# The second group of each ConvFFN: its up projection as seven block products instead of two direct tiles

## The chip, the cores and the metric

The kernel runs on one core of one Trainium2 chip. The metric is the device time of one execution in microseconds; the runs of a kernel are told by their median.

## What is computed

A two-layer decoder trunk on 512 tokens of width 1024, in float32. Each layer adds a mixer and then a gated ConvFFN to the residual stream. The ConvFFN is what the change touches:

```python
def gated_conv_ffn(x, w_gate, w_up, conv_w, conv_b, w_down):
    g = jnp.einsum('bsd,df->bsf', x, w_gate)          # 1024 -> 2816
    g = causal_dwconv3(g, conv_w) + conv_b            # width 3, along the tokens
    up = jnp.einsum('bsd,df->bsf', x, w_up)           # 1024 -> 2816
    return jnp.einsum('bsf,fd->bsd', jax.nn.silu(g) * up, w_down)

for layer in range(2):
    h = h + mixer(rms_norm(h, norm_mix[layer]))
    hn = rms_norm(h, norm_ffn[layer])
    h = h + gated_conv_ffn(hn, w_ffn_gate[layer], w_ffn_up[layer], ...)
return rms_norm(h, final_norm)
```

## The kernel before

**Precision.** Every float32 operand of a matmul is held as a high and a low part, and each product is three matmuls: high by high, high by low, low by high (`mm3`, lines 139 to 141; line 631 for block products). The high part is a rounding copy on ScalarE. The low part is source minus high: a subtraction on VectorE (`parts`, lines 134 and 135; `halves`, lines 640 and 641), or ScalarE writes the negated high part and a DMA from POOL's queue adds the source to it (`summed`, lines 126 to 128; lines 602 to 604 in `normalize`).

**Groups and parts.** The hidden width 2816 is 22 tiles of 128 columns. A group `f` is two neighbouring tiles of the gate and of the up projection. Groups 0 and 2 are followed by the down projection of tiles 0 and 1 (called `d` in layer 0, `dn` in layer 1); groups 4, 6, 8 and so on follow, with a down projection of four tiles behind every one or two groups, as `PARTS` says. The activations of group 2 are thus used one part later.

**Group 0** (`hidden(0)`) starts before the norm's root is known: it multiplies by the input scaled with the gain alone, tile by tile over the 8 blocks of 128 input channels in the order `PAIRS` (0, 4, 1, 5, 2, 6, 3, 7), and its results are multiplied by the root when they leave PSUM. In the middle of it TensorE sums the squares (`rstd_tokens`) and spreads the root over the partitions by four transposes (`rstd_spread`, line 211; ScalarE's copy is line 214). Then `normalize(kp)`, for the four pairs of input blocks (kp, kp + 4), writes the normalized input over `hg` and makes four combinations `t` of its quarters (lines 579 to 604). Their high and low parts are `t23` and `t41`. `rest()` then evacuates group 0: root, convolution (one scaled copy on ScalarE, line 512, two steps on VectorE, line 514), silu (line 520), multiplication with up (line 569), split into `a_hi` and `a_lo` (lines 253 and 255).

**Group 2** is direct too, on the normalized input: the gate's two tiles first, then the two up tiles, 48 matmuls of 512 columns each. Its weights come through `pair_weights`.

**Groups from 4 on** (`both`) use Strassen's scheme in its seven-product form. The matrix of 1024 input channels by two tiles is cut in halves both ways, and so is the input (channel half by token half). Seven block products, each 4 x 3 matmuls of 256 columns (`multiply`), replace eight. Each needs a stationary block of the weights or a combination of them (`a11` for product 1, `s12` for 5 and 6, `s34` for 7 and 3, the lower half of the weights for 2 and 4) and a moving block of the input or of its combinations: products 6 and 7 read `t23`, 4 and 5 read `t41`. The products are added partly in PSUM and partly in `kept` or in padded rows.

**What sets the order.** A framework takes the program's order as priority and orders every engine's instructions itself when the kernel is built. Buffers turn round in pools: four for raw weights (`raw`), six each for high and low parts (`whi`, `wlo`), three for sums (`sum`), seven PSUM banks for matmuls (`mm`) and one beside (`aux`). A tile waits for a buffer until all readers of an earlier one are done. Loads of weights go through SP's queue.

Of the kernel before, what the change touches and what calls it, by code (L numbers as in the profile page):

```python
# [8 lines left out]
F32 = mybir.dt.float32  # L9
# [3 lines left out]
ALU = mybir.AluOpType  # L13
PSUM = bass.MemoryType.PSUM

P = 128
D = 1024
S = 512
NK = D // P
# [11 lines left out]
def tile_trunk(ctx: ExitStack, tc: tile.TileContext, x, norm_mix, norm_ffn, final_norm,  # L31
# [3 lines left out]
    nc = tc.nc  # L35
    x = x[0]
# [8 lines left out]
    def mm_bank(name):  # L45
        return ps_mm.tile([P, 512], F32, tag="mm", name=name)
# [91 lines left out]
    def mm3(ps, lhs, rhs, start, stop):  # L138
        nc.tensor.matmul(ps, lhs[0], rhs[0], start=start, stop=False)  # L139
        nc.tensor.matmul(ps, lhs[0], rhs[1], start=False, stop=False)  # L140
        nc.tensor.matmul(ps, lhs[1], rhs[0], start=False, stop=stop)  # L141
# [27 lines left out]
    def hg_k(k):  # L169
        return hg[k][0], hg[k][1]  # L170

    class Norm:
# [6 lines left out]
        def add(self, k):  # L179
            g = self.gain(k)  # L180
            nc.scalar.activation(hg[k][0], h[k], AF.Copy, scale=g)
            nc.vector.scalar_tensor_tensor(hg[k][1], h[k], g, hg[k][0].bitcast(F32),
                                           op0=ALU.mult, op1=ALU.subtract)
            self.square(k)
# [90 lines left out]
    def padded_tile():  # L275
        turn[0] += 1
        return padded[turn[0] % NPADDED]
# [205 lines left out]
    HALF = S // 2  # L483
    NP = NK // 2
    PAIRS = [k for i in range(NP) for k in (i, i + NP)]

    def ffn_weights(layer, f, order):
        cs = slice(f * P, (f + 2) * P)
        return {(key, half): fetch(
            (w_ffn_gate if key == "g" else w_ffn_up)[layer][half * 512 : (half + 1) * 512, cs]  # L490
            .rearrange("(k p) c -> p k c", p=P), 4, 256, f"{key}{layer}_{f}_{half}")
            for key, half in order}

    class Ffn:
# [42 lines left out]
                ch[key, half] = (summed if key in by_dma else parts)(raw, 4, 2 * P, name)  # L537
            return ch

        def direct(self, f, normed, sets, ch, before=lambda i, j: None):  # L540

            layer = self.layer
            banks = {}
            for js in sets:
                for i, k in enumerate(PAIRS):
                    for j in js:
                        before(i, j)
                        hi, lo = ch["gu"[j // 2], i // 4]
                        c = slice((j % 2) * P, (j % 2 + 1) * P)
                        if j not in banks:  # L550
                            banks[j] = mm_bank(f"gu{layer}_{f}_{j}")
                        mm3(banks[j], (hi[:, i % 4, c], lo[:, i % 4, c]), hg_k(k),
                            i == 0, i == NK - 1)

            def evacuate():
                r = self.r
                gates = []
                for j in range(2):
                    t = padded_tile()
                    if normed:  # L560
                        nc.scalar.copy(t[:, 2:], banks[j])
                    else:
                        nc.vector.tensor_tensor(t[:, 2:], banks[j], r, ALU.mult)
                    s = self.silu(self.conv(t, f + j), f + j)
                    if not normed:
                        nc.gpsimd.tensor_tensor(s, s, r, ALU.mult)
                    gates.append(s)
                for j, s in enumerate(gates):
                    nc.vector.tensor_tensor(s, banks[2 + j], s, ALU.mult)
                    self.act(f + j, s)  # L570

            return evacuate

        def normalize(self, kp):

            n, r = f"{self.layer}_{kp}", self.r
            x = self.ap.tile([P, 2, S], F32, tag="sum", bufs=3, name=f"x{n}")
            for i, k in enumerate((kp, kp + NP)):
                nc.vector.scalar_tensor_tensor(x[:, i, :], h[k], self.prm("ffn", k), r,
                                               op0=ALU.mult, op1=ALU.mult)  # L580

            def halves(dst, src):
                nc.scalar.activation(dst[0], src, AF.Copy)
                nc.vector.tensor_tensor(dst[1], src, dst[0].bitcast(F32), ALU.subtract)

            halves(hg[kp], x[:, 0, :])
            halves(hg[kp + NP], x[:, 1, :])
            b11, b12 = x[:, 0, :HALF], x[:, 0, HALF:]
            b21, b22 = x[:, 1, :HALF], x[:, 1, HALF:]
            t = self.ap.tile([P, 4, HALF], F32, tag="sum", bufs=3, name=f"t{n}")  # L590
            nc.vector.tensor_tensor(t[:, 1, :], b22, b12, ALU.subtract)
            nc.vector.tensor_tensor(t[:, 0, :], t[:, 1, :], b11, ALU.add)
            nc.vector.tensor_tensor(t[:, 3, :], b12, b11, ALU.subtract)
            nc.vector.tensor_tensor(t[:, 2, :], b21, t[:, 0, :], ALU.subtract)
            self.t23[kp] = self.sums(kp)
            t41 = self.ap.tile([P, 2, 2, HALF], F32R, name=f"t41_{n}")
            self.t41[kp] = t41[:, 0], t41[:, 1]
            for (hi, lo), src in ((self.t23[kp], t[:, :2, :]), (self.t41[kp], t[:, 2:, :])):
                if kp < 2:
                    halves((hi, lo), src)  # L600
                    continue
                nc.scalar.activation(lo, src, AF.Copy, scale=-1.0)
                nc.gpsimd.dma_start(lo, src, accum_op=ALU.add)
                nc.scalar.activation(hi, src, AF.Copy)
# [34 lines left out]
        def halves(self, hi, lo, src):  # L639
            nc.scalar.activation(hi, src, AF.Copy)  # L640
            nc.vector.tensor_tensor(lo, src, hi.bitcast(F32), ALU.subtract)  # L641

        def both(self, f):

# [74 lines left out]
        def hidden(self, f, before=lambda i, j: None):  # L719
            if f == 0:  # L720
                def first(i, j):
                    before(i, j)
                    if (i, j) == (1, 0):
                        self.norm.rstd_tokens()
                    elif (i, j) == (2, 2):
                        self.r = self.norm.rstd_spread()

                ch = self.pair_weights(0, [("g", 0), ("u", 0), ("g", 1), ("u", 1)])
                rest = self.direct(0, False, (range(4),), ch, first)
                self.ch = self.pair_weights(2, [("g", 0), ("g", 1), ("u", 0), ("u", 1)], "g")  # L730
                for kp in range(NP):
                    self.normalize(kp)
                rest()
            elif f == 2:
                self.direct(2, True, ((0, 1), (2, 3)), self.ch)()
            else:
                self.both(f)

# [229 lines left out]
    n = mixer0()  # L968
    n = ffn0(n)
    n = mixer1(n)  # L970
# [31 lines left out]
```

## Time and profile before

| what | value |
|---|---|
| median of 3 runs | 1000.65 us (1000.1 to 1001.06) |
| the profiled execution | 1000.02 us, of it span 998.3 us |
| granted TensorE clock, mean | 0.998 |
| TensorE busy | 986.5 us (99%), 5835 matmuls |
| VectorE / ScalarE / POOL busy | 699.9 / 522.7 / 100.6 us |
| HBM read and written | 98.42 and 2.10 MB |

Times in rows are microseconds from the span's start unless marked ns. A timeline row is start, duration, engine, line, operation, output<-inputs, shape and count; in brackets stands the idle time before it and what ended it. In names the layer and buffer numbers are mostly left out: `gu` is a direct bank of groups 0 and 2, `u_4a` the bank `a` of group 4's up products, `d` and `dn` the down projections. Durations of neighbouring instructions on one engine overlap a little, so the distance between two starts is the price of one.

### The profile page before, as it was taken

Reading aid. Unit: us, or ns where it says so; the run is one execution under the profiler, and the core shown is the slowest. Engines: PE = TensorE matmul, PEld = TensorE weight load, DVE = VectorE, ACT = ScalarE, POOL = GpSimd, SP = SyncE. Lnnn points to the kernel's source line nnn. Section 1 sums busy time; section 2 is a strip of 40 time slices with the busy share of each in tenths; the row PEclk is TensorE's granted clock in tenths of the full one; section 3 lists DMA queues with packets and bytes.
Section 4 is the critical chain, followed back from the end, with each engine's and each line's share of the span. In section 5 each row is a group of like instructions: output and inputs, shape, how many; then the busy total and the mean of one; then the engine's idle time right before and its main releaser. Section 6 shows DMA issues by size and latency. Waiting matters only on the chain.

```text
span 998.3 us, 14727 instructions
## 1 busy us (share of the span) xinstructions
PE 986.5 (99%) x5835; PEld 874.5 (88%) x5835; DVE 699.9 (70%) x1057; ACT 522.7 (52%) x775; POOL 100.6 (10%) x117
## 2 busy tenths in 40 slices
PE   8999999999999999999999999999999999999997
PEld 6888888898999989999888888888989899898995
DVE  5977457967785877858943645389668868688677
ACT  6522345744653746537655444675536366363663
POOL 3032030300000000000300001202000010000100
PEclk9999999999999999999999999999999999999999
DMA  7532225454554645546433223434535446354442
GB/s 233 184 105 85 85 85 127 107 150 124 130 145 106 175 121 132 144 106 184 132 127 106 63 86 104 100 91 118 158 95 145 141 112 184 94 141 146 119 115 84
DMA packets 81904, 124.53 MB, mean 125 GB/s; under 512 B 4292, under 2 KB 53676, under 8 KB 81836
## 3 DMA queue, kind: packets, MB, share of 16 engines
q1 hardware_dynamic: 73580, 98.96, 31.6%
q0 software_dynamic: 6912, 23.07, 12.9%
q10 hardware_dynamic: 1344, 1.58, 0.5%
q8 instruction: 45, 0.74, 0.3%
q14 instruction: 23, 0.19, 0.1%
HBM read 98.42 MB, written 2.10 MB: 101 GB/s over the span
## 4 chain that ended last, share of the span: by engine, by line
PE 92%; DVE 4%; DMA 2%; ACT 1%; issue 0%; SPq 0%; POOL 0%; DVEq 0%; ACTq 0%; POOLq 0%
PE d L139 4%; PE d L140 4%; PE d L141 4%; PE dn L139 4%; PE dn L140 3%; PE dn L141 3%; PE gu L139 3%; PE gu L141 3%; PE gu L140 3%; PE u L141 1%; PE oo L141 1%; PE oo L139 1%; PE u L140 1%; PE u L139 1%; PE oe L140 1%; PE oe L139 1%
## 5 line engine op out<-in xcount | busy, mean ns | idle before, releaser
L139 PE MATMUL dn<-whi_dn,a_hi 128*128 128x512 f32 x176 | 68.7, 390 | 0.0
L140 PE MATMUL d<-a_lo,whi_d 128*128 128x512 f32 x176 | 68.6, 390 | 0.0
L140 PE MATMUL dn<-wlo_dn,a_hi 128*128 128x512 f32 x176 | 68.6, 390 | 0.0
L141 PE MATMUL d<-a_hi,wlo_d 128*128 128x512 f32 x176 | 68.5, 389 | 0.0
L514 DVE SCALAR_TENSOR_TENSOR c<-rows,prm,c 128x512 f32<-128x512 f32 x88 | 67.5, 791 | 0.0
L141 PE MATMUL dn<-whi_dn,a_lo 128*128 128x512 f32 x176 | 67.3, 390 | 0.0
L139 PE MATMUL d<-a_hi,whi_d 128*128 128x512 f32 x176 | 66.9, 390 | 0.0
L127 POOL DMA_DIRECT2D wlo_g<-raw_g x22 | 19.1, 868 | 382.3 <-ACT wlo_g L126 350.7
L931 DVE TENSOR_TENSOR y<-dn,y 128x512 f32<-128x512 f32 x48 | 32.3, 685 | 22.8 <-PE dn L141 22.3
L126 ACT ACTIVATE wlo_g<-raw_g 128x1024 fp32r<-128x1024 f32 x22 | 23.2, 1055 | 42.4 <-PE dn L140 42.4
L135 DVE TENSOR_TENSOR wlo_u<-raw_u,whi_u 128x1024 fp32r<-128x1024 f32 x16 | 19.6, 1223 | 34.2 <-ACT whi_u L134 34.1
L520 ACT ACTIVATE s<-c,prm 128x512 f32<-128x512 f32 x44 | 30.9, 717 | 22.7 <-DVE c L514 22.6
L640 ACT ACTIVATE whi_s12u<-s12u 128x1024 fp32r<-128x1024 f32 x18 | 18.9, 1050 | 43.1 <-PE d L140 33.7
L641 DVE TENSOR_TENSOR wlo_s34u<-s34u,whi_s34u 128x1024 fp32r<-128x1024 f32 x18 | 22.1, 1226 | 26.1 <-ACT whi_s34u L640 26.1
L141 PEld LDWEIGHTS dn<-whi_dn,a_lo 128*128 128x128 f32 x176 | 33.0, 188 | 7.5 <-DVE a_lo L255 0.2
L140 PEld LDWEIGHTS d<-a_lo,whi_d 128*128 128x128 f32 x176 | 33.1, 188 | 7.2 <-DVE a_lo L255 0.2
L139 PEld LDWEIGHTS dn<-whi_dn,a_hi 128*128 128x128 f32 x176 | 33.1, 188 | 7.1 <-ACT a_hi L253 0.2
L139 PEld LDWEIGHTS d<-a_hi,whi_d 128*128 128x128 f32 x176 | 32.8, 188 | 7.0
L298 DVE TENSOR_TENSOR h<-d,h 128x512 f32<-128x512 f32 x48 | 32.5, 685 | 9.2 <-PE d L141 9.2
L141 PEld LDWEIGHTS d<-a_hi,wlo_d 128*128 128x128 f32 x176 | 33.0, 188 | 6.7
L140 PEld LDWEIGHTS dn<-wlo_dn,a_hi 128*128 128x128 f32 x176 | 33.1, 188 | 6.5
L135 DVE TENSOR_TENSOR wlo_dn<-raw_dn,whi_dn 128x1024 fp32r<-128x1024 f32 x22 | 26.8, 1221 | 12.8 <-ACT whi_dn L134 12.8
(1201 smaller groups left out, 3412.3 us busy)
## 6 DMA issues: line engine op xcount, KB each, us to landing
raw_g<-in_w_ffn_gate_dram SPq DMA_DIRECT2D x36, 512.0 KB, 4.0
raw_u<-in_w_ffn_up_dram SPq DMA_DIRECT2D x36, 512.0 KB, 4.0
wlo_g<-raw_g POOLq DMA_DIRECT2D x22, 512.0 KB, 4.8
raw_d<-in_w_ffn_down_dram SPq DMA_DIRECT2D x22, 512.0 KB, 4.4
raw_dn<-in_w_ffn_down_dram SPq DMA_DIRECT2D x22, 512.0 KB, 4.7
wlo_u<-raw_u POOLq DMA_DIRECT2D x18, 512.0 KB, 4.7
raw_oe<-in_w_out_even_dram SPq DMA_DIRECT2D x8, 512.0 KB, 3.5
raw_g<-in_w_ffn_gate_dram SPq DMA_DIRECT2D x16, 256.0 KB, 2.9
```

The source lines that it names most:

```text
L126: nc.scalar.activation(lo, raw, AF.Copy, scale=-1.0)
L127: nc.gpsimd.dma_start(lo, raw, accum_op=ALU.add)
L135: nc.vector.tensor_tensor(lo, raw, hi.bitcast(F32), ALU.subtract)
L139: nc.tensor.matmul(ps, lhs[0], rhs[0], start=start, stop=False)
L140: nc.tensor.matmul(ps, lhs[0], rhs[1], start=False, stop=False)
L141: nc.tensor.matmul(ps, lhs[1], rhs[0], start=False, stop=stop)
L298: nc.vector.tensor_tensor(h[k], ps, h[k], ALU.add)
L514: nc.vector.scalar_tensor_tensor(c, t[:, i : S + i], prm("cf", i * NF + ft), c, op0=ALU.mult, op1=ALU.add)
L520: nc.scalar.activation(s, c, AF.Silu, bias=self.prm("bf", ft))
L640: nc.scalar.activation(hi, src, AF.Copy)
L641: nc.vector.tensor_tensor(lo, src, hi.bitcast(F32), ALU.subtract)
L931: nc.vector.tensor_tensor(dst, ps, dst, ALU.add)
```

## The change

The up projection of group 2 is computed in the seven products; the gate stays direct. The new function `up_only` loads the two halves of the up weights, makes the stationary blocks (`a1` for products 1 and 2, `s12u`, `s34u`, and `a22` for 4), and then orders TensorE's work: the gate's first six input blocks, products 1 and 2, one gate block of three matmuls, products 6, 5 and 7, the gate's last nine matmuls, and products 4 and 3. The results are collected in `kept`. `direct` now serves group 0 alone. In `normalize` the low parts of `t` for pairs 2 and 3 are made on VectorE and those of pairs 0 and 1 by DMA, which is the other way round than before. The root is spread before tile (2, 0) of group 0 instead of (2, 2). `multiply`, `unit` and `moving` are the functions that the later groups use.

```diff
--- before.py
+++ after.py
@@ -537,33 +537,28 @@
                 ch[key, half] = (summed if key in by_dma else parts)(raw, 4, 2 * P, name)
             return ch
 
-        def direct(self, f, normed, sets, ch, before=lambda i, j: None):
+        def direct(self, f, ch, before):
 
             layer = self.layer
             banks = {}
-            for js in sets:
-                for i, k in enumerate(PAIRS):
-                    for j in js:
-                        before(i, j)
-                        hi, lo = ch["gu"[j // 2], i // 4]
-                        c = slice((j % 2) * P, (j % 2 + 1) * P)
-                        if j not in banks:
-                            banks[j] = mm_bank(f"gu{layer}_{f}_{j}")
-                        mm3(banks[j], (hi[:, i % 4, c], lo[:, i % 4, c]), hg_k(k),
-                            i == 0, i == NK - 1)
+            for i, k in enumerate(PAIRS):
+                for j in range(4):
+                    before(i, j)
+                    hi, lo = ch["gu"[j // 2], i // 4]
+                    c = slice((j % 2) * P, (j % 2 + 1) * P)
+                    if j not in banks:
+                        banks[j] = mm_bank(f"gu{layer}_{f}_{j}")
+                    mm3(banks[j], (hi[:, i % 4, c], lo[:, i % 4, c]), hg_k(k),
+                        i == 0, i == NK - 1)
 
             def evacuate():
                 r = self.r
                 gates = []
                 for j in range(2):
                     t = padded_tile()
-                    if normed:
-                        nc.scalar.copy(t[:, 2:], banks[j])
-                    else:
-                        nc.vector.tensor_tensor(t[:, 2:], banks[j], r, ALU.mult)
+                    nc.vector.tensor_tensor(t[:, 2:], banks[j], r, ALU.mult)
                     s = self.silu(self.conv(t, f + j), f + j)
-                    if not normed:
-                        nc.gpsimd.tensor_tensor(s, s, r, ALU.mult)
+                    nc.gpsimd.tensor_tensor(s, s, r, ALU.mult)
                     gates.append(s)
                 for j, s in enumerate(gates):
                     nc.vector.tensor_tensor(s, banks[2 + j], s, ALU.mult)
@@ -596,7 +591,7 @@
             t41 = self.ap.tile([P, 2, 2, HALF], F32R, name=f"t41_{n}")
             self.t41[kp] = t41[:, 0], t41[:, 1]
             for (hi, lo), src in ((self.t23[kp], t[:, :2, :]), (self.t41[kp], t[:, 2:, :])):
-                if kp < 2:
+                if kp >= 2:
                     halves((hi, lo), src)
                     continue
                 nc.scalar.activation(lo, src, AF.Copy, scale=-1.0)
@@ -639,6 +634,77 @@
         def halves(self, hi, lo, src):
             nc.scalar.activation(hi, src, AF.Copy)
             nc.vector.tensor_tensor(lo, src, hi.bitcast(F32), ALU.subtract)
+
+        def up_only(self, f, ch):
+
+            layer, ap, n = self.layer, self.ap, f"{self.layer}_{f}"
+            raws = ffn_weights(layer, f, [("u", 0), ("u", 1)])
+            r0, r1 = raws["u", 0][0], raws["u", 1][0]
+            stat = {}
+            w = self.unit(f"a1_{n}")
+            self.halves(w[0][:, 0], w[1][:, 0], r0[:, :, :P])
+            self.halves(w[0][:, 1], w[1][:, 1], r1[:, :, :P])
+            stat[1], stat[2] = (tuple(x[:, i] for x in w) for i in range(2))
+            s12, s34 = (ap.tile([P, 2, 4, P], F32, tag="sum", bufs=3, name=f"{x}u_{n}")
+                        for x in ("s12", "s34"))
+            nc.vector.tensor_tensor(s12[:, 0], r0[:, :, P:], r1[:, :, P:], ALU.add)
+            nc.vector.tensor_tensor(s12[:, 1], s12[:, 0], r0[:, :, :P], ALU.subtract)
+            w = self.unit(f"s12u_{n}")
+            self.halves(*w, s12)
+            stat[5], stat[6] = (tuple(x[:, i] for x in w) for i in range(2))
+            nc.vector.tensor_tensor(s34[:, 0], r0[:, :, :P], r0[:, :, P:], ALU.subtract)
+            nc.vector.tensor_tensor(s34[:, 1], r1[:, :, :P], s12[:, 1], ALU.subtract)
+            w = self.unit(f"s34u_{n}")
+            self.halves(*w, s34)
+            stat[7], stat[3] = (tuple(x[:, i] for x in w) for i in range(2))
+            w = self.unit(f"a22_{n}")
+            self.halves(w[0][:, 0], w[1][:, 0], r1[:, :, P:])
+            stat[4] = w[0][:, 0], w[1][:, 0]
+
+            banks = {}
+
+            def gate(i, js):
+                k = PAIRS[i]
+                for j in js:
+                    if j not in banks:
+                        banks[j] = mm_bank(f"g{j}{n}")
+                    hi, lo = ch["g", i // 4]
+                    c = slice(j * P, (j + 1) * P)
+                    mm3(banks[j], (hi[:, i % 4, c], lo[:, i % 4, c]), hg_k(k),
+                        i == 0, i == NK - 1)
+
+            def product(p):
+                return self.multiply(banks, f"u{n}", p, stat[p])
+
+            kept = ap.tile([P, 3, HALF], F32, tag="kept", bufs=1, name=f"kept{n}")
+
+            def add(i, ps):
+                nc.vector.tensor_tensor(kept[:, i, :], ps, kept[:, i, :], ALU.add)
+
+            for i in range(6):
+                gate(i, range(2))
+            nc.scalar.copy(kept[:, 0, :], product(1))
+            add(0, product(2))
+            gate(6, (0,))
+            nc.scalar.copy(kept[:, 1, :], product(6))
+            p5 = product(5)
+            nc.scalar.copy(kept[:, 2, :], product(7))
+            add(2, p5)
+            gate(6, (1,))
+            gate(7, range(2))
+            s = []
+            for j in range(2):
+                t = padded_tile()
+                nc.scalar.copy(t[:, 2:], banks[j])
+                s.append(self.silu(self.conv(t, f + j), f + j))
+            p4 = product(4)
+            nc.vector.tensor_tensor(s[1][:, HALF:], kept[:, 2, :], s[1][:, HALF:], ALU.mult)
+            nc.vector.tensor_tensor(s[1][:, :HALF], p4, s[1][:, :HALF], ALU.mult)
+            self.act(f + 1, s[1])
+            add(1, product(3))
+            s0 = s[0].rearrange("p (a b) -> p a b", a=2)
+            nc.vector.tensor_tensor(s0, kept[:, :2, :], s0, ALU.mult)
+            self.act(f, s[0])
 
         def both(self, f):
 
@@ -722,17 +788,17 @@
                     before(i, j)
                     if (i, j) == (1, 0):
                         self.norm.rstd_tokens()
-                    elif (i, j) == (2, 2):
+                    elif (i, j) == (2, 0):
                         self.r = self.norm.rstd_spread()
 
                 ch = self.pair_weights(0, [("g", 0), ("u", 0), ("g", 1), ("u", 1)])
-                rest = self.direct(0, False, (range(4),), ch, first)
-                self.ch = self.pair_weights(2, [("g", 0), ("g", 1), ("u", 0), ("u", 1)], "g")
+                rest = self.direct(0, ch, first)
+                self.ch = self.pair_weights(2, [("g", 0), ("g", 1)], "g")
                 for kp in range(NP):
                     self.normalize(kp)
                 rest()
             elif f == 2:
-                self.direct(2, True, ((0, 1), (2, 3)), self.ch)()
+                self.up_only(2, self.ch)
             else:
                 self.both(f)
```

## The prediction

> **What bounds the kernel now.** I read the page first, then TensorE's waits, then the windows of the two FFN openings, then the timelines of the engines there.
>
> ```profile
> span 998.3 us, 14727 instructions
> PE 986.5 (99%) x5835; PEld 874.5 (88%) x5835; DVE 699.9 (70%) x1057; ACT 522.7 (52%) x775; POOL 100.6 (10%) x117
> PE 92%; DVE 4%; DMA 2%; ACT 1%; issue 0%; SPq 0%; POOL 0%; DVEq 0%; ACTq 0%; POOLq 0%
> ```
>
> TensorE is busy 986.5 of 998.3 us and makes 92% of the chain that ended last. The page warns that matmuls are pipelined, so a busy row alone proves little; the list of waits is the better witness. In the FFNs it has one entry:
>
> ```profile
> PE u_20e L631 <- DVE wlo_s12u L641: 0.3, 1, 0.3
> ```
>
> So matmul time counts one to one, and a saving elsewhere counts nothing. But the entry names what comes next: TensorE waiting for VectorE's low part of `s12u`. The windows from the first normalized tile to the start of group 4, in layer 0 and layer 1, show how near that is (busy times of PE, PEld, DVE, ACT, POOL in that order):
>
> ```profile
> 157.80:204.64 46.84, 46.84 (x209) 38.76 (x207) 46.81 (x75) 31.37 (x46) 7.70 (x7) 1.00 0.43 103
> 651.50:698.51 47.01, 47.01 (x210) 38.93 (x209) 46.98 (x75) 31.27 (x46) 7.72 (x7) 1.00 0.44 104
> ```
>
> VectorE is as full as TensorE there (46.81 of 46.84 us), ScalarE is idle 15.5 us. The granted clock is 1.00, so no clock effect enters. The page's 70% for VectorE is an average that hides this. The changed group lies in just these windows.
>
> **What TensorE loses.** Group 2 runs gate first, then up; these are the starts of the gate, of the up projection, of the down projection behind it, and of two products in group 4:
>
> ```profile
> 172.00 0.39 PE L139 MATMUL gu<-hgh,whi_g 128*128 128x512 f32 x1
> ...
> 182.88 0.39 PE L139 MATMUL gu<-hgh,whi_u 128*128 128x512 f32 x1
> ...
> 193.76 0.39 PE L139 MATMUL d<-a_hi,whi_d 128*128 128x512 f32 x1
> ...
> 206.07 0.28 PE L631 MATMUL u_4a<-hgh,whi_a 128*128 128x256 f32 x1
> ...
> 207.51 0.28 PE L631 MATMUL g_4e<-t,whi_s12g 128*128 128x256 f32 x1
> ```
>
> The up projection is 2 tiles x 8 input blocks x 3 = 48 matmuls of 512 columns, from 182.88 to 193.76: 10.88 us, 0.227 each. The change replaces them with 7 products of 4 x 3 = 12 matmuls of 256 columns. One such product takes 207.51 - 206.07 = 1.44 us (0.120 a matmul; half of 0.227 would be 0.113, so narrow matmuls give a little back). Seven take 10.08 us. Saved: 0.80 us a layer, **1.60 us in all**. The gate's 48 matmuls stay and are only moved among the products, so the width changes six times. The one such change in the trace, from the down projection into group 4, costs nothing: 0.23 before the first narrow matmul and 0.11 after it.
>
> ```profile
> 204.41 0.39 PE L141 MATMUL d<-a_hi,wlo_d 128*128 128x512 f32 x1
> 204.64 0.28 PE L631 MATMUL g_4a<-hgh,whi_a 128*128 128x256 f32 x1
> 204.75 0.28 PE L631 MATMUL g_4a<-hgl,whi_a 128*128 128x256 f32 x1
> ```
>
> The Trainium skill, "TensorE: Matmul & The Clock Gate", section "Back-to-back issue gap", gives the isolated gap as columns over 2.4 GHz plus 2.5 ns; my estimate from that page is 10.36 us against 9.17, or 2.4 us saved over both layers. The rows above disagree with it on both widths (227 and 120 ns against 216 and 109), so the trace decides and this result gets no chance.
>
> **What moves the start.** The spread of the norm's root goes from before tile (2, 2) to before (2, 0), six matmuls or 1.36 us earlier.
>
> ```profile
> 153.56 0.16 DVE L243 SCALAR_TENSOR_TENSOR rc_f0t<-ms_f0t,rc_f0t 128x4 f32<-128x4 f32 x1
> ...
> 156.57 0.60 PE L211 MATMUL ssr_f<-ident,rc_f0t 128*128 128x128 f32 x4
> ...
> 157.83 1.42 DVE L579 SCALAR_TENSOR_TENSOR x<-h,prm,rstd_f 128x512 f32<-128x512 f32 x2 [4.10 <-ACT rstd_f L214]
> 159.16 0.42 DVE L593 TENSOR_TENSOR t<-x 128x256 f32<-128x256 f32 x1
> ```
> ```profile
> 647.02 0.16 DVE L243 SCALAR_TENSOR_TENSOR rc_f1t<-ms_f1t,rc_f1t 128x4 f32<-128x4 f32 x1
> ...
> 650.28 0.60 PE L211 MATMUL ssr_f<-ident,rc_f1t 128*128 128x128 f32 x4
> ```
>
> The transposes move to 155.21, and their columns are done at 153.72; in layer 1 to 648.92 against 647.18. TensorE waits for neither, so it costs nothing; the gates' multiplications behind them only slide. VectorE, which sat idle 4.10 us for the root, starts normalizing at 156.47 instead of 157.83.
>
> **What VectorE gets.** Back-to-back starts give the real price of each shape:
>
> ```profile
> 180.53 2.34 DVE L135 TENSOR_TENSOR wlo_d<-raw_d,whi_d 128x1024 fp32r<-128x1024 f32 x2
> 182.80 0.68 DVE L641 TENSOR_TENSOR wlo_a<-raw_g,whi_a 128x512 fp32r<-128x512 f32 x1
> 183.40 1.77 DVE L514 SCALAR_TENSOR_TENSOR c<-rows,prm,c 128x512 f32<-128x512 f32 x1
> ...
> 192.45 0.68 DVE L660 TENSOR_TENSOR s12g<-raw_g,raw_g 128x512 f32<-128x512 f32 x1
> 193.05 0.68 DVE L667 TENSOR_TENSOR s34g<-raw_g 128x512 f32<-128x512 f32 x1
> ...
> 227.23 0.42 DVE L712 TENSOR_TENSOR s<-kept,s 128x256 f32<-128x256 f32 x1
> 227.57 0.42 DVE L713 TENSOR_TENSOR s<-u_4a,s 128x256 f32<-128x256 f32 x1
> ```
>
> That is 1.14 us for 1024 elements, 0.60 for 512, 0.34 for 256, and 0.67 for a scaled one (159.16 - 157.83, over two). The up weights' two low parts of 1024 go (-2.28). In come `a1` 2 x 0.60, the sums `s12` and `s34` 4 x 0.60, their lows 2 x 1.14, `a22` 0.60: 6.48. Three additions into `kept` and the split multiplications add 3 x 0.34 + (0.34 + 0.34 + 0.60 - 1.20) = 1.10. Sum: **+5.3 us** a layer. The low parts of the pairs only change places: four of 512 elements leave pairs 0 and 1 and four come to pairs 2 and 3, net zero, and their four DMAs on POOL's queue come earlier, ahead of the gate scalings of group 0. The reason lies in when the old ones landed:
>
> ```profile
> 180.46 0.85 POOL L603 DMA_DIRECT2D t<-t  x1 [0.19 <-issue]
> ```
> ```profile
> t<-t POOLq DMA_DIRECT2D x6, 256.0 KB, 3.8
> ```
>
> 180.46 + 3.8 is 184.3, while the new product 5 starts near 185.2 (172.00 + 36 gate matmuls of 0.227, products 1 and 2, three gate matmuls, product 6). With the DMA on pairs 0 and 1, all land many us ahead; I put this at nothing, covered by the gate's 8.2 us.
>
> ScalarE gets a high part for each new low part, less than VectorE's sum, plus three quarter-bank copies; its 15.5 us idle in the window hide these. If that cover failed, VectorE's lows would wait with them and the price would be that of the rivals. On the DMA queue of SP the same two loads of up weights stand at the same place, but both buffers are now read until `a22`; the group 4 loads behind them wait for that.
>
> **Does VectorE's addition reach TensorE?** The tight place is the one in the wait list, the low part of `s12u` for group 4, against its first reader:
>
> ```profile
> 205.01 1.23 DVE L641 TENSOR_TENSOR wlo_s12u<-s12u,whi_s12u 128x1024 fp32r<-128x1024 f32 x1
> ...
> 700.44 1.21 DVE L641 TENSOR_TENSOR wlo_s12u<-s12u,whi_s12u 128x1024 fp32r<-128x1024 f32 x1
> ```
> ```profile
> 210.63 0.28 PE L631 MATMUL u_4e<-t,wlo_s12u 128*128 128x256 f32 x1
> ...
> 704.34 0.28 PE L631 MATMUL u_4e<-t,wlo_s12u 128*128 128x256 f32 x1
> ```
>
> The slack now is 4.39 us in layer 0 (210.63 - 206.24) and 2.69 in layer 1. VectorE comes 5.3 - 1.36 = 3.94 later and the reader 0.80 earlier, 4.74 in all. If VectorE's order stays and nothing else fills, TensorE waits 0.35 and 2.05 us, 2.4 together: the upper bound of this term. Its lower bound is zero, and I take 0.1, because neither order is fixed. On VectorE the `s34g` sums and low (2 x 0.60 + 1.14 = 2.34) stand ahead of it, though product g7 comes two products later. And TensorE's own stream already steps around late operands, as in group 8:
>
> ```profile
> 271.23 0.24 PE u_8e L631 x2
> ...
> 271.59 1.54 PE g_8a L631 x12
> ...
> 273.37 0.48 PE g_8b L631 x4
> 273.85 1.20 PE u_8e L631 x10
> ```
>
> Here ten matmuls of the u5 product stand behind those of g2 and g7. Those two products are 2.88 us of cover, more than 2.05.
>
> **Sum.** -1.60 + 0.1 = -1.5 us. On the profiled execution, 1000.02 us with span 998.3 (1.72 us around it), that gives span 996.8 and 998.5 us. The median of the runs, 1000.65, lies 0.63 above that execution; forecast **999.1 us** (-0.15%). A measurement of this kernel can tell about 0.2%, 2.0 us, from no change, so the likeliest case lies inside "same", near its edge.
>
> **Rivals.** *B, no cover:* VectorE keeps its order and TensorE its own. Then the 2.4 us of waits stand and the time is 1000.65 - 1.6 + 2.4 = 1001.4. For it: VectorE's full windows. Against: group 8's rows. Chance 0.17.
>
> *C, slower: VectorE falls behind inside group 2, at `s34u` for product 7.* From 156.47 it has normalization (8 x 0.67, 16 x 0.34, 12 x 0.60: 18.0), group 0's tail (6 x 0.60 and 4 x 0.67, of which two take 1.77 beside POOL's scaling as at 183.40 and below: 8.5), `a1`, `s12`, `s34` and two lows (5.9): 32.4, up to 188.9. If the down weights' lows (2.27) go first too, 191.1. Product 7 starts at 186.6 and reads the low at 186.9: late by 4.2 at most. The gate's last nine matmuls cover 2.04; a wait of up to 2.2 a layer stays, 1000.65 - 1.6 + 4.4 = 1003.5. It decides from 1.8 a layer on (1002.7).
>
> ```profile
> 187.62 1.78 DVE L514 SCALAR_TENSOR_TENSOR c<-rows,prm,c 128x512 f32<-128x512 f32 x1
> ```
>
> Against: group 0's last multiplications and low parts (2.4) and the down weights' lows are wanted only when the down projection begins, near 193, and can go behind. Without them the low comes by 186.5. Chance 0.15.
>
> *D, PSUM:* seven banks turn round; the up tiles' last bank is freed only by the product-4 multiplication, after a silu that starts 7.2 us later than now (the gate ends at 190.1, not 182.9). Today that place has room:
>
> ```profile
> 195.46 1.28 DVE L569 TENSOR_TENSOR s<-gu,s 128x512 f32<-128x512 f32 x2
> ```
>
> The multiplications end at 196.7; the sixth down tile starts at 193.76 + 5 x 1.36 = 200.6. After the change the first bank of the products is wanted by the fifth down tile, 192.96 + 5.44 = 198.4, and from 190.1 eight steps in a row of 0.60 to 0.67 (copies, conv and silu, ScalarE's taken as long as VectorE's) and the two half multiplications (0.68) end near 196. A miss of 1 us a layer gives 1001.1. Chance 0.06, inside "same".
>
> **How the numbers follow.** Forecast 0.62, B 0.17, C 0.15, D 0.06. The runs spread from 1000.10 to 1001.06, so a true -1.5 may show as more than -2.0: I give 0.20 of the forecast's 0.62 to faster, the rest, 0.42, to same. B and D are same but for 0.03 that go to slower. So faster 0.20, same 0.62, slower 0.18. The low end is 999.1 less 0.7 for the spread and the last 0.3 us wait; the high end takes in B and the spread, and stops short of C.
>
> **What would show it.** Right: an up block of products of 1.44 us; the down projection and group 4 start 0.8 us earlier against the start of the FFN, in both layers; TensorE's waits stay below 1 us; VectorE full until near the u5 product. B shows as waits at `wlo_s12u`, C at `wlo_s34u` of group 2, D at VectorE's multiplications before a down tile. Products longer than 1.44 us, or a VectorE window with idle stretches for loads, would prove the sum wrong.

## The result: slower by 1.6%, and the profile after

The changed kernel takes 1016.99 us in the median of six runs (1013.34 to 1020.62), the kernel before 1000.79 beside it: a ratio of 1.0159 (95% interval 1.0135 to 1.0183). The forecast was 999.1, with a range that took in rival B's 1001.4 and the spread of the runs and stopped short of rival C. The profiled execution took 1017.46 us, of it a span of 1015.7.

The page of the changed kernel, its span, busy times and the chain that ended last:

```profile
span 1015.7 us, 14885 instructions
...
PE 992.8 (98%) x5907; PEld 881.8 (87%) x5907; DVE 710.5 (70%) x1079; ACT 527.9 (52%) x787; POOL 105.7 (10%) x117
...
PE 78%; DVE 7%; issue 7%; DMA 6%; ACT 1%; SPq 0%; POOL 0%; DVEq 0%; POOLq 0%; ACTq 0%
```

TensorE was to be busy 1.6 us less and is busy 6.3 us more. Its share of the chain falls from 92% to 78%. TensorE's waits (total, times, longest) have new entries:

```profile
PE u_2a L626 <- ACT kept L686: 4.4, 2, 2.2
PE u_4b L626 <- DMA wlo_u<-raw_u: 3.6, 2, 2.9
PE wst L838 <- POOL ws L831: 1.8, 1, 1.8
...
PE u_8b L626 <- DMA wlo_u<-raw_u: 1.0, 1, 1.0
```

Starts of the stages in the two timelines give the account. "Opening" is from the first matmul of the FFN (in layer 1 from its first transpose) to the first of group 4; group 4 ends at its down projection.

| stage | before | after | difference |
|---|---|---|---|
| opening, layer 0 | 56.72 | 59.91 | +3.19 |
| group 4, layer 0 | 20.15 | 25.71 | +5.56 |
| rest of layer 0 | 270.87 | 271.45 | +0.58 |
| mixer 1 | 142.42 | 143.73 | +1.31 |
| opening, layer 1 | 60.26 | 63.40 | +3.14 |
| group 4, layer 1 | 20.16 | 21.59 | +1.43 |
| rest of layer 1, up to the last matmuls | 250.33 | 252.28 | +1.95 |

These add up to 17.16. The span is 17.4 longer; the part ahead of layer 0's FFN, in which the change has no share, took 0.5 more, and the very end 0.2 less. The table's last row is mostly the waits at `u_8b` (1.0) and `u_20b` (0.5).

**Group 2.** TensorE in the changed kernel, from the gate's block ahead of product 6 to product 7:

```profile
184.00 0.39 PE L141 MATMUL g<-hgh,wlo_g 128*128 128x512 f32 x1
184.23 0.40 PE L626 MATMUL u_2e<-t,whi_s12u 128*128 128x256 f32 x2
186.82 0.38 PE L626 MATMUL u_2a<-t23h,whi_s12u 128*128 128x256 f32 x1 [2.20 <-ACT kept L686]
...
188.06 0.41 PE L626 MATMUL u_2a<-t23h,whi_s12u 128*128 128x256 f32 x1
188.27 0.41 PE L626 MATMUL u_2a<-t23l,whi_s12u 128*128 128x256 f32 x1
...
191.05 0.28 PE L626 MATMUL u_2a<-t23h,whi_s34u 128*128 128x256 f32 x1
```

Two matmuls of product 5 were ready, then TensorE stood 2.20 us before product 6. And behind the wait the starts lie 0.21 us apart instead of 0.12, up to about 190.5. The windows over that stretch, and over the same stretch behind the wait in group 4 (busy times of PE, PEld, DVE, ACT, POOL, then the granted clock):

```profile
186.82:190.62 3.80, 3.80 (x19) 3.80 (x20) 2.63 (x4) 2.71 (x4) 2.56 (x1) 0.55 0.02 4
224.80:228.20 3.40, 3.40 (x19) 3.40 (x18) 0.42 (x1) 0.00 (x0) 0.00 (x0) 0.52 0.87 269
```

PE reads "busy" all through, at half the clock. From 186.82 to 191.05 stand 22 matmuls, 2.64 us at full clock and 4.23 here: 1.59 us lost, beside 2.35 at the gap (184.23 to 186.82 less the two). Together 3.94, and less the 0.80 saved by the products (each still 1.43 to 1.44 us where nothing waits) this is the +3.19.

Why product 6 was late stands on ScalarE and VectorE:

```profile
181.78 1.06 ACT L635 ACTIVATE whi_s12u<-s12u 128x1024 fp32r<-128x1024 f32 x1 [1.07 <-DVE s12u L651]
183.49 1.06 ACT L635 ACTIVATE whi_s34u<-s34u 128x1024 fp32r<-128x1024 f32 x1 [0.65 <-DVE s34u L656]
...
186.42 0.35 ACT L686 COPY kept<-u_2a 128x256 f32<-128x256 f32 x1
```
```profile
167.17 1.41 DVE L574 SCALAR_TENSOR_TENSOR x<-h,prm,rstd_f 128x512 f32<-128x512 f32 x2 [1.17 <-DMA t<-t]
...
181.06 0.69 DVE L651 TENSOR_TENSOR s12u<-s12u,raw_u 128x512 f32<-128x512 f32 x1
181.78 1.67 DVE L656 TENSOR_TENSOR s34u<-raw_u,s12u 128x512 f32<-128x512 f32 x1
...
185.30 1.21 DVE L636 TENSOR_TENSOR wlo_s12u<-s12u,whi_s12u 128x1024 fp32r<-128x1024 f32 x1
```
```profile
180.18 2.72 POOL L561 TENSOR_TENSOR s<-s,rstd_f 128x512 f32<-128x512 f32 x1 [12.37 <-ACT s L520]
```

Product 6 writes the same bank as product 1, so it needs that bank copied out. Product 1 was done at 182.1, but its copy (L686) stands in ScalarE's queue behind the high part of `s34u` and three shorter operations, and starts at 186.42. VectorE finishes the low part of `s12u` at 186.51: both come some 2 us late for a reader at 184.5, and the list of waits names only the last. VectorE had lost time twice before that. It stood 1.17 us up to 167.17, because the pairs' `t` stay in their buffers until the DMA has read them. And one 512-wide operation (`s34u`) took 1.67 us instead of 0.60: POOL's multiplication runs from 180.18 to 182.90, and VectorE's ends 0.55 after it. The two sums ahead of it began inside POOL's row too and took their 0.60 each; POOL's, at 2.72 us, seems to have waited for them in its turn. The Trainium skill, "SBUF — State Buffer", section "SBUF: two separate sides", says that the two engines lock a shared pair of ports for a whole instruction, for VectorE with two inputs in SBUF against a POOL operation that reads SBUF; these rows agree.

**Group 4.** Here the low parts made by DMA from POOL's queue are late. The issues on POOL, first before, then after:

```profile
207.17 0.86 POOL L127 DMA_DIRECT2D wlo_u<-raw_u  x1 [8.14 <-ACT rows L691]
```
```profile
216.77 0.86 POOL L127 DMA_DIRECT2D wlo_u<-raw_u  x1 [6.22 <-ACT wlo_u L126]
```

The time to landing, from the DMA issues between 190 and 230 us, before and then after, and TensorE's reader, after:

```profile
wlo_u<-raw_u POOLq DMA_DIRECT2D x1, 512.0 KB, 4.5
```
```profile
wlo_u<-raw_u POOLq DMA_DIRECT2D x1, 512.0 KB, 7.2
```
```profile
224.05 0.39 PE L626 MATMUL u_4b<-hgh,wlo_u 128*128 128x256 f32 x1 [2.89 <-DMA wlo_u<-raw_u]
```

It is issued 8.43 us after group 4 begins (208.34) instead of 2.53 (204.64), behind `s12u`, `s34g` and their high parts, and lands after 7.2 us instead of 4.5. TensorE waits 2.89 us and again pays about 1.7 us of half clock. In layer 1 the same wait is 0.74 us and no slow stretch follows, which is most of the difference between +5.56 and +1.43.

### The profile page after: what moved, and what is told of

It reads as the page before. It is cut to its first block, busy times and chain, and to the rows that moved or that the text cites. A ratio compares the mean times of both kernels' runs of the same rounds, so it can differ in the third digit from the quotient of the medians.

```text
span 1015.7 us, 14885 instructions
## 1 busy us (share of the span) xinstructions
PE 992.8 (98%) x5907; PEld 881.8 (87%) x5907; DVE 710.5 (70%) x1079; ACT 527.9 (52%) x787; POOL 105.7 (10%) x117
## 3 DMA queue, kind: packets, MB, share of 16 engines
q10 hardware_dynamic: 1344, 1.58, 0.5%
## 4 chain that ended last, share of the span: by engine, by line
PE 78%; DVE 7%; issue 7%; DMA 6%; ACT 1%; SPq 0%; POOL 0%; DVEq 0%; POOLq 0%; ACTq 0%
PE d L139 3%; PE d L140 3%; PE d L141 3%; PE dn L139 3%; PE dn L140 3%; PE dn L141 3%; DMA wlo_u<-raw_u 3%; PE u L139 1%; PE u L141 1%; PE oo L139 1%; PE oo L141 1%; PE oe L141 1%; PE oe L139 1%; PE u L140 1%; PE oo L140 1%
## 5 line engine op out<-in xcount | busy, mean ns | idle before, releaser
L514 DVE SCALAR_TENSOR_TENSOR c<-rows,prm,c 128x512 f32<-128x512 f32 x88 | 63.4, 745 | 0.0
L636 DVE TENSOR_TENSOR wlo_s34u<-s34u,whi_s34u 128x1024 fp32r<-128x1024 f32 x20 | 24.5, 1224 | 27.4 <-ACT whi_s34u L635 27.4
L635 ACT ACTIVATE whi_s12u<-s12u 128x1024 fp32r<-128x1024 f32 x20 | 21.0, 1052 | 39.0 <-PE d L140 33.7
L135 DVE TENSOR_TENSOR wlo_u<-raw_u,whi_u 128x1024 fp32r<-128x1024 f32 x12 | 14.7, 1224 | 34.2 <-ACT whi_u L134 34.1
L195 POOL TENSOR_TENSOR ssq_f<-ssq_f,sq_f 128x512 f32<-128x512 f32 x12 | 16.3, 1357 | 179.8 <-ACT sq_f L194 144.9
```

The costliest lines, as they stand in the source:

```text
L195: nc.gpsimd.tensor_tensor(self.ssq, self.ssq, sq, ALU.add)
L514: nc.vector.scalar_tensor_tensor(c, t[:, i : S + i], prm("cf", i * NF + ft), c, op0=ALU.mult, op1=ALU.add)
```

## The experiments

All ratios are against the kernel before. "Opening" and "group 4" with a plus are differences from before in layers 0 and 1, as in the table above.

**1. The small parts alone.** The kernel before with the root spread earlier and the pairs' low parts swapped, group 2 direct.

```diff
-                if kp < 2:
+                if kp >= 2:
...
-                elif (i, j) == (2, 2):
+                elif (i, j) == (2, 0):
```

> The kernel before with only the two small parts of the change: the root spread before tile (2, 0), and the low parts of t for pairs 2 and 3 on VectorE, those of pairs 0 and 1 by DMA; group 2 stays direct. If the loss comes from the block products (theory 1 and 2 below), this is the kernel before within 0.1%: 1000 to 1001.5 us. If the swapped low parts cost by themselves (their DMAs hold two of the three sum buffers and VectorE stands idle 1.2 us), TensorE would show waits in groups 2 or 4 and the time would be 1003 or more.

Measured: 1001.51 us, ratio 1.0005 (0.9996 to 1.0015). VectorE stands idle for as long as 4.75 us, because the pairs' `t` stay in the `sum` buffers until their DMA is done:

```profile
173.00 0.42 DVE L593 TENSOR_TENSOR t<-x 128x256 f32<-128x256 f32 x1 [4.75 <-DMA t<-t]
```

TensorE feels little of it: it waits 0.35 us once, the openings are 0.78 and 0.02 longer, and the time is the same. The loss needs the products.

**2. The products alone.** The changed kernel without those two edits.

> The changed kernel without those two parts: block products for up, low parts and spread as before. Theory 1 (ScalarE's queue): product 6 waits because the copy of product 1 out of the same PSUM bank stands in ScalarE's queue behind high parts that wait for VectorE; in this kernel's order the copy stands ahead of s34u's high part, so the wait shrinks from 2.2 to under 0.5 us in each layer and, with the half clock behind each wait, some 2 x 3.5 us come back: about 1010. Theory 2 (VectorE is simply late): VectorE starts 1.4 us later here, so the waits grow and the time is 1017 or more.

Measured: 1014.54 us, ratio 1.0135 (1.012 to 1.015).

```profile
PE g_4b L626 <- DMA wlo_g<-raw_g: 3.4, 2, 1.7
PE wst L838 <- POOL ws L831: 1.8, 1, 1.8
PE u_2a L626 <- DVE wlo_s12u L636: 1.8, 2, 0.9
PE u_2a L626 <- ACT whi_s34u L635: 1.7, 2, 0.8
```

So the products cost 13.5 us alone. The wait in group 2 is split in two of 0.9 and 0.8, and these openings are only 1.6 longer than before: no slow clock behind them. Group 4 is 4.2 to 4.3 longer in both layers. The time lies between those of the two theories. It also shows that the small parts are not free beside the products: with them the openings are 3.2 longer, and without them 1.6. The times do not tell the two kernels apart (1.012 to 1.015 against 1.0135 to 1.0183).

**3. Product 6 in a bank of its own.** Its bank begins a new sum. This leaves product 1 out of product 6's result, and product 6 out of those of 7 and 4; the work and its order are the same.

```diff
-                return self.multiply(banks, f"u{n}", p, stat[p])
+                return self.multiply(banks, f"u{n}", p, stat[p], {6: "c"}.get(p))
```

> The changed kernel with product 6 of group 2 in a PSUM bank of its own, so that it no longer waits for the copy of product 1. Theory 1: the wait of 2.2 us and the slow clock behind it go in both layers, about 2 x 3.9 us: 1009. Theory 2: the low part of s12u came from VectorE at 186.5, hardly before the copy at 186.8, so the wait is there again under VectorE's name: 1016 to 1017.

Measured: 1015.51 us, ratio 1.015 (1.0135 to 1.0165).

```profile
PE u_4b L626 <- DMA wlo_u<-raw_u: 4.4, 2, 3.7
PE u_2c L626 <- DVE wlo_s12u L636: 3.9, 2, 1.9
```

The wait is 1.93 us instead of 2.20 and now names VectorE. The bank and the copy alone are not the cause: that theory falls.

**4. The gate's last nine matmuls ahead of product 6.** They are 2.04 us of work where TensorE stood 2.2.

```diff
-            gate(6, (0,))
+            gate(6, range(2))
+            gate(7, range(2))
             nc.scalar.copy(kept[:, 1, :], product(6))
...
-            gate(6, (1,))
-            gate(7, range(2))
```

> The changed kernel with all of the gate's last matmuls ahead of product 6 (nine matmuls, 2.04 us, moved from behind product 7). Both theories: the wait before product 6 is covered but for some 0.2 us and the clock stays full, so 2 x 3.9 us come back: 1009. If the wait only moves on (the low part of s34u came at 188.3, and no gate matmuls are left to cover it), a wait of 1 to 2 us appears at product 7 and the time is 1013 to 1017.

Measured: 1015.86 us, ratio 1.0157 (1.014 to 1.0174).

```profile
PE u_2a L626 <- ACT kept L690: 3.5, 2, 1.8
PE u_4b L626 <- DMA wlo_u<-raw_u: 2.7, 2, 2.0
```

The wait moves on to product 7. ScalarE and VectorE lag over the whole group; this change of TensorE's order only moves the place.

**5. The gating multiplication on VectorE instead of POOL.**

```diff
-                    nc.gpsimd.tensor_tensor(s, s, r, ALU.mult)
+                    nc.vector.tensor_tensor(s, s, r, ALU.mult)
```

> Group 0's gate times the root goes from POOL to VectorE (two multiplications of 512, about 1.2 us more for VectorE a layer). Theory POOL (VectorE is late at product 6 because its 512-wide operation beside POOL's takes 1.67 instead of 0.60 us and it then waits 1.17 us for POOL): about 2.2 us go and 1.2 come, the low part of s12u lies about 1 us earlier, the wait ahead of product 6 falls from 2.2 to 1.2 us or less in each layer, and the time to 1012 to 1015. Theory budget (only the amount of VectorE work counts): the wait grows by 1.2 us a layer, 1018 to 1020. In this kernel's order the copy of product 1 stands earlier on ScalarE, so if that copy alone were the bound, the wait would vanish: 1009 to 1010.

Measured: 1011.43 us, ratio 1.011 (1.0093 to 1.0127). VectorE gets 1.2 us more work, and the wait falls:

```profile
PE g_4b L626 <- DMA wlo_g<-raw_g: 2.7, 2, 1.4
PE u_4b L626 <- DMA wlo_u<-raw_u: 1.8, 2, 1.6
PE wst L838 <- POOL ws L831: 1.8, 1, 1.8
PE u_2a L626 <- DVE wlo_s12u L636: 1.6, 2, 0.8
```

The openings are 0.62 longer than before in each layer instead of 3.2. The budget theory (1018 to 1020) falls. The low part of `s12u` is done 36.95 us after the start of the FFN, against 38.08 after the change; where `s34u`'s sum took 1.67 beside POOL, the gating multiplication now takes 0.60:

```profile
183.77 1.21 DVE L636 TENSOR_TENSOR wlo_s12u<-s12u,whi_s12u 128x1024 fp32r<-128x1024 f32 x1
```

The copy of product 1 stands earlier here too. But in experiment 3 product 6 needs no copy, and with POOL's multiplication kept it waits 1.93 for a low part that is done at 38.08. Experiment 9 has the copy about as early as here and waits 1.87, though with 0.6 us of `a22`'s low part ahead. What is left lies in group 4: +4.12 and +3.98.

**6. Work in the place of the wait.** Nine spare matmuls into the spare bank ahead of product 6.

```diff
             gate(6, (0,))
+            fill = aux_bank(f"fill{n}")
+            for i in range(9):
+                nc.tensor.matmul(fill, hg[0][0][:, :P], hg[0][0], start=i == 0, stop=i == 8)
```

> Nine spare matmuls of 512 columns (2.04 us) into the spare bank stand ahead of product 6, so TensorE works where it waited 2.2 us. Theory clock (a wait of about 2 us is followed by some 4 us in which matmuls take 0.21 instead of 0.12 us, which costs 1.6 us more): the granted clock stays 1.0 behind product 6, group 2 ends 1.6 us earlier in each layer in spite of the spare work, the time is 1012 to 1014.5 (the wait of group 4 and its slow stretch stay). Rival (the slow stretch comes from something else, such as late operands of the next products): the slow stretch stays, the time is the same 1016 to 1018.

Measured: 1011.8 us, ratio 1.0101 (1.0086 to 1.0117). TensorE does 4.1 us more work in all, and the kernel is some 5 us faster than the changed one. In the windows the granted clock stays full:

```profile
183.32:187.12 3.80, 3.44 (x20) 2.73 (x19) 3.80 (x5) 3.60 (x7) 1.45 (x1) 1.00 0.18 64
185.90:187.40 1.50, 1.50 (x12) 1.50 (x13) 1.42 (x2) 1.50 (x2) 1.50 (x1) 1.00 0.04 11
```

The clock part of the theory holds: no gap of over 1.2 us, no slow stretch. The sum came out for another reason than expected: at full clock TensorE runs into ScalarE's next copies (1.1 and 0.5 us), and the openings are 4.1 longer than before, not shorter than after. The gain is in group 4, which is back at +0.34 and +0.23. The rebuilt order there has the second products behind all of `u_4e`, and the first load of down weights is issued at 198.55 instead of 207.66, ahead of the low part's DMA, which lands in 4.5 us again.

**7. Less work for VectorE.** The first down projection's low parts by DMA, which is 2.27 us off VectorE in each layer.

```diff
-                hi, lo = weights(
+                hi, lo = (summed if name == "d0_0" else parts)(*fetch(
```

> The low parts of the first down projection's weights are made by DMA instead of on VectorE, which takes two operations of 1024 (2.27 us) from VectorE in each layer. Theory VectorE (its total up to the low part of s12u decides): that part comes about 2 us earlier, TensorE's wait ahead of product 6 falls to at most 1.8 us (the copy on ScalarE then sets it) and the time falls by 1 to 8 us, 1009 to 1016. Rival (ScalarE's queue in order decides, with the copy behind a high part that waits for s34u): s34u also comes earlier with VectorE, so only if POOL's multiplication holds s34u does the wait stay at 2.2 us and the time at 1016 to 1018.

Measured: 1019.52 us, ratio 1.0181 (1.0151 to 1.021).

```profile
PE u_2a L626 <- ACT kept L686: 4.3, 2, 2.2
...
PE dn L140 <- DMA wlo_dn<-raw_dn: 1.4, 1, 1.4
```

A miss: the wait is unchanged. Those low parts stood behind the tight place already (at 191.56 in the changed kernel), and their DMA makes a new wait. What counts is VectorE's work ahead of the late part, not its total.

**8. Experiments 5 and 7, and group 4's DMA low parts issued first.**

> Three at once: group 0's gating on VectorE, the first down projection's low parts by DMA, and group 4's two low parts by DMA issued ahead of the other work of that group. Theory (the loss is made of late VectorE work in group 2, the late low part of the up weights in group 4, and the slow clock behind each wait): the wait ahead of product 6 falls below 0.8 us and u_4b's below 1 us, the time is 1000 to 1006. Rival (the loads of group 4's weights themselves come too late, since both up buffers are read until a22): u_4b still waits 2 us or more and the time stays at 1008 to 1012.

Measured: 1009.11 us, ratio 1.0076 (1.0061 to 1.0091). `u_4b` waits no more, and group 4 is +0.72 and +0.71. The down projections wait for the new DMA instead (1.5 to 1.8 a layer), and the openings grow by 1.8 and 2.4 us against experiment 5, which takes back over half of the 3.4 and 3.3 won in group 4. The time is in the rival's range, but the rival's reason, late loads with `u_4b` waiting, did not come.

**9. `a22` early.** Its parts right behind those of `a1`, to free the raw up buffers sooner.

> The high and low part of a22, the last reader of the second raw up buffer of group 2, are made right behind those of a1; nothing else is changed. Theory loads (group 4 waits since its raw weights, and behind them the raw down weights, are fetched late, so that the three down loads run beside the low parts' DMA, which then takes 7.2 us instead of 4.5): the loads of group 4 start about 5 us earlier, the DMA of wlo_u lands in 4.5 to 5 us, u_4b waits less than 1 us and group 4 takes 20.2 to 21.5 us instead of 25.7; VectorE has 0.6 us more ahead of the low part of s12u, so the wait in group 2 stays about 2 us. In all 1010 to 1013. Rival (ScalarE and VectorE reach the low parts of group 4 late whatever the loads do): group 4 still takes 24 to 26 us, the time is 1016 to 1019.

Measured: 1014.47 us, ratio 1.0135 (1.0115 to 1.0155).

```profile
PE u_4b L626 <- DMA wlo_u<-raw_u: 3.8, 2, 3.3
PE u_2a L626 <- DVE wlo_s12u L636: 3.7, 2, 1.9
```

The load moved only from 190.74 to 189.24, so this does not test the load theory as meant, and the time lies between the two ranges; layer 0's group 4 is as long as after (25.80).

**10. Experiment 5 with group 4's DMA low parts issued first.**

```diff
+            early = {key: summed(*raws[key, 1]) for key in "gu"} if f == 4 else {}
             for key in "gu":
...
-                hi, lo = summed(*raws[key, 1])
+                hi, lo = early[key] if early else summed(*raws[key, 1])
```

> The gating multiplication on VectorE as in the run before, and group 4's two DMA low parts issued ahead of the other work of that group. In the run with the multiplication alone group 2 (from the start of the FFN to group 4) took 0.6 us more than before in each layer and group 4 took 4.1 more. Theory: that 4.1 is the late DMA of wlo_g and wlo_u and the slow clock behind their waits; with the DMA about 8 us earlier group 4 takes 20.2 to 21 us, and the time is 1001.0 + 2 x 0.6 + 2 x 0.5 + 1.3 (the wait at wst in mixer 1) = 1004.5, at least 1003, at most 1006.5. Rival (VectorE's low part of s12u for group 4 is late too and takes the wait over): group 4 takes 22.5 us or more, 1008 or more.

Measured: 1006.04 us, ratio 1.0053 (1.0036 to 1.0069).

```profile
PE wst L839 <- POOL ws L832: 1.8, 1, 1.8
PE u_2a L626 <- DVE wlo_s12u L636: 1.7, 2, 0.8
```
```profile
201.22 0.85 POOL L127 DMA_DIRECT2D wlo_u<-raw_u  x1 [1.66 <-ACT wlo_u L126]
```

The DMA leaves 4.8 us before group 4 begins (206.04), `u_4b` no longer waits, and group 4 falls from +4.12 and +3.98 to +1.03 and +0.73. The late issue was the cause there.

**11. The same with `a22` early.**

> As the run with the multiplication and the early DMA, and with a22's parts made early as well. Theory loads: group 4 as short as before (20.2 to 20.5), but product 6's low part 0.6 us later, so the wait in group 2 grows by 0.3 to 0.6 us a layer, or more if it passes the point where the clock drops: 1004 to 1008. Rival (the loads do not matter once the DMA is issued early): group 4 as in the other run, the time 1 to 2 us above it.

Measured: 1006.74 us, ratio 1.006 (1.0045 to 1.0075). The first raw up load of group 4 goes out 4.5 us earlier (186.52 against 191.04), group 4 is the same within 0.35, and the openings are 0.42 longer: once the DMA is issued early, these loads do not decide.

**12. All together**, with the gate early and the pairs' low parts as before.

> Everything that should help at once: the gating multiplication on VectorE, a22's parts early, the gate's last nine matmuls ahead of product 6, the low parts of the pairs as in the kernel before, group 4's DMA low parts early. Theory (VectorE is late by 1 to 2 us and nothing else): the gate's 2.04 us cover it, group 2 becomes 0.3 to 0.8 us shorter than before in each layer, group 4 at most 0.5 us longer, wst 1.3 us longer: 1000 to 1002.5. Rival (VectorE is short of time over the whole window, so that the wait moves to product 7 or to the down projection): 1004 to 1010.

Measured: 1005.48 us, ratio 1.0048 (1.0033 to 1.0063).

```profile
PE wst L837 <- POOL ws L830: 1.8, 1, 1.8
...
PE u_4e L626 <- ACT whi_s12u L635: 1.2, 2, 0.8
...
PE d L139 <- ACT whi_d L134: 0.5, 1, 0.5
PE dn L139 <- ACT whi_dn L134: 0.5, 1, 0.5
```

The theory (1000 to 1002.5) misses; the time is in the rival's range, VectorE short of time over the whole window. The best of them is still slower than before: openings +0.54 and +0.52, group 4 +1.08 and +0.62, mixer 1 +1.36. The product's 0.80 a layer is there, but 1.3 is lost again around it, of which the waits in the list name 0.5. No version beat the kernel before.

## Why the prediction was wrong

- **The saving was right.** A product takes 1.43 to 1.44 us and the changes of width cost nothing visible.
- **The tight place was the wrong one: this is the step that failed first.** The prediction named group 4's `s12u` and, in rival C, `s34u` for product 7 behind the gate's nine matmuls. Product 6 stands ahead with three gate matmuls (0.7 us) for cover. By the prediction's own list, rival C's 188.9 less the `s34` low and sums (1.14 and 1.20) puts `s12u`'s low at 186.6, against product 6's start near 183.7 (172.00 + 8.17 + 2.88 + 0.68). Measured were 186.51 and 184.2. The numbers held the sign, but only the operand of the later product was compared. That the two times of the low part agree so well is luck: the list has neither the 1.17 us for the pairs' `t` nor the 1.07 beside POOL nor the `s34u` sums ahead of it, and it counts about as much work that went behind or ran undisturbed.
- **ScalarE "hidden by 15.5 us of idle" failed.** An average hides what stands ahead of what. The copy of product 1 waited behind a high part that waited for VectorE, and came at 186.42 for a product that was ready at 184.5. Experiment 3 shows that it was not alone, VectorE's low part being as late.
- **"The low parts only change places" and "at nothing" held only beside the direct group** (experiment 1). VectorE idles for the `sum` buffers, 1.17 us in the changed kernel, and beside the products the openings are 1.6 us shorter without the small parts (experiment 2).
- **VectorE's prices were those of undisturbed shapes.** The sum of work was right (+5.3 a layer; VectorE's busy time grew by 10.6 in both), and not what counted (5 and 7). POOL's gating held one 0.60 us operation for 1.67 ahead of the low part; the prediction had that doubling in its rows and charged it to the convolution, not to the new operations that would stand in its place.
- **"Granted clock 1.00, so no clock effect enters" failed.** It was read from a kernel without gaps. A wait of 2.2 us cost 3.9, of which 1.6 were half clock.
- **Group 4 was priced by VectorE alone.** Its waits are for POOL's DMA (`wlo_u`, `wlo_g`), whose source passes through ScalarE behind that same work. The prediction said that group 4's loads would wait, and gave no price. TensorE's "stepping around late operands" does not help when the low part is issued 5.9 us later.
- **Rival C had the right sign and engine, at 2.9 us (1003.5 against 1000.65) instead of 16.2.** It lacked group 4, the clock, and the waits downstream.
- **Open:** mixer 1's +1.3. In every kernel with the products but the filler's, `ws` is loaded 1.3 us later at the end of layer 0 (3.8 us after the mixer's first matmul instead of 2.5). In just these kernels the last residual addition comes 1.3 us later too (at 3.1 instead of 1.8). So a changed order of the residual additions is the likely reason, and no run isolates it. How much of group 4's first delay is VectorE's backlog and how much the rebuilt order is open too: the filler's order removes the wait with VectorE's work unchanged.

## What to carry to other kernels

When an engine is full, list every new operand against its first reader, product by product, and look at the first that is late, not the last; ask also which copy frees a bank, and what stands ahead of it in its engine's order. Price a wait on TensorE of some 1.4 us or more at its length and up to 1.7 us more. Work that swells one group shows in the next as late DMA: follow the group's issue times past its end.

## What the runs showed of the hardware

- A gap on TensorE can halve the granted clock, each time for 3.41 us, and the gap need not be long. The trace records when the granted clock changes. In the changed kernel it is half from 187.10, 224.65 and 692.28 us; these starts lie 11 and 137 times 3.413 us apart, and in every run the changes lie on such a raster. So what seems to count is how much idle time falls into one window of the raster, not the length of a gap. Two windows of experiment 5, each with the one behind it (the columns as above):

```profile
210.74:214.15 3.41, 1.85 (x14) 1.43 (x13) 2.72 (x4) 3.41 (x4) 0.46 (x1) 1.00 1.00 213
214.16:217.57 3.41, 3.41 (x18) 3.41 (x18) 1.30 (x2) 1.39 (x3) 0.38 (x1) 0.50 0.82 213
```
```profile
719.33:722.74 3.41, 1.94 (x16) 1.94 (x17) 1.17 (x3) 0.03 (x1) 0.00 (x0) 1.00 0.69 201
722.74:726.16 3.42, 3.42 (x31) 3.42 (x30) 0.43 (x2) 1.47 (x3) 0.00 (x0) 1.00 0.81 283
```

  In the first TensorE is idle 1.56 us, a wait of 1.39 and shorter ones, and the next window runs at half clock. In the second it is idle 1.47, because the wait of 1.62 is cut in two by the raster, and nothing follows. In the FFNs of all runs, every window with 1.56 us or more of idle was followed by a slow one, and none with less than 1.5. Idle time is not the whole rule: 1.73 to 1.84 us ahead of the `wst` transposes, within one window in eight kernels, were never followed. That a wait between some 1.4 and 1.8 us is sometimes paid and sometimes not fits the spread of the changed kernel's runs (7.3 us against 2.0 before), which no run isolates. The Trainium skill, "TensorE: Matmul & The Clock Gate", section "Part 1: The HAM clock gate (the "warmup" mystery)", puts activity into free-running windows of about 3.4 us: the raster and the length of the slow stretch agree. It has the clock drop after an idle window of about 3.4 us; here 1.56 us of idle in one window were enough, so the measurement decides.
- POOL's own multiplication took 2.72 and 2.79 us after, and 1.81 and 1.58 before, for the same shape, beside other VectorE work.
